# A hybrid encoder layer on one core: the high parts of the mixer's weights asked for one chunk further ahead, and another order inside the seven-product pairs

## The chip, the cores and the metric

One core of a Trainium2 chip. The metric is the device time of one execution in microseconds (us); lower is better. A difference under 0.3% is about what a measurement of this kernel can't tell from no change.

## The reference: what is computed

One encoder layer on 512 tokens of width 1024, all in float32:

```
h = rms_norm(x, g_mix);  z = h @ w_in            # split into latents, gates, values
a = mla(...)                                     # 4 heads of latent attention
r = hgrn2(...)                                   # 4 heads of a gated recurrence, both directions
x = x + concat(a, r) @ w_o
h = rms_norm(x, g_ffn)
x = x + (silu(h @ w_gate) * (h @ w_up)) @ w_down # inner width 2816 = 22 tiles of 128
x = x + sigmoid(rms_norm(x, g_ple) @ w_ple_gate) * (p @ w_ple_proj)
```

## The kernel before

Every float32 operand is kept as a high part (float32r) and a low part, the rest of it, and every product is three matmuls (`mm3`, L141 to L144): high by high, high by low, low by high. A weight therefore has to be loaded and split before TensorE can use it.

**Mixer.** The layer up to the residual of `w_o` runs as two streams of instructions that `merge` interleaves: a latency stream (attention, then the recurrence) and a dense stream (projections of 1024-column chunks of weights, the output projection, the embedding's projection). The dense stream takes its chunks from `wnext` (L602), which keeps `AHEAD` = 3 chunks prepared beyond the one in use. From the third chunk on a chunk is prepared without VectorE: GpSimd's queue (POOL) starts a DMA that casts the float32 weight into the high part `whi` (L155), ScalarE writes the negated high part into `wlo` (L156), and a second DMA of POOL's queue adds the float32 weight to it (L157). `whi` and `wlo` have `WB` = 4 buffers each, so a chunk's high part can be asked for when TensorE is done with the chunk four places before. Attention runs beside it; its softmax needs ScalarE (L557), and TensorE transposes the probabilities after it (L571). POOL also computes the small powers of every norm (L175).

**Feed-forward.** 22 pairs of a gate tile and an up tile. The first four are plain (`pair_plain`). After each of them `block_sums(c)` makes, from the normalised input, the sums that the other 18 pairs multiply by: in each half-width product the 1024 by 512 input is a 2 by 2 block matrix, and `pair_seven` gets the four blocks of its output from seven products instead of eight. A pair loads four raw blocks (A11 and A12 from `w_gate`, A21 and A22 from `w_up`, 256 KB each, L1102 on SyncE's queue, SP), forms four sums S1 to S4 of them on VectorE (`total`, L1112), splits all seven left operands (`operand`: high part on ScalarE L135, low part on VectorE L136) and runs seven products of twelve 128x256 matmuls (`product`), in the order A11, A12, S2, S1, S3, S4, A22. Between pairs run the down projections (`down`, tile `dn`).

**Buffers.** All 128x512 tiles of SBUF come from one list of numbered slots (`Slots`): `get` takes the slot that was put back longest ago, `put` appends. So the code alone fixes whose slot a tile inherits, and a load into it waits for that tile's last reader. There are `SLOTS` = 74, and 22 more (`SLOTS2`) once the mixer's weight buffers are closed.

**Order.** The order of the instructions of each engine is fixed at build time by the framework's scheduler, from its own times; each engine then runs in that order and stands wherever the next instruction is not ready.

Of the kernel before, what the change touches and what calls it, by code (L numbers as in the profile page):

```python
# [9 lines left out]
F32R = mybir.dt.float32r  # L10
I32 = mybir.dt.int32
AF = mybir.ActivationFunctionType
ALU = mybir.AluOpType
AX = mybir.AxisListType

P = 128
# [4 lines left out]
EPS = 1e-6  # L21
QK_SCALE = 192 ** -0.5
FPARTS = (4, 4, 4, 4, 3, 3)
SLOTS = 74
SLOTS2 = 22
DAHEAD = 2

# [1 line left out]
AHEAD = 3  # L29
WB = 4  # L30
# [4 lines left out]
LO_DVE = 2  # L35
# [76 lines left out]
def v3(t, a, b=None):  # L112

    return t.rearrange("p (a b) -> p a b", a=a)
# [3 lines left out]
def layer_kernel(ctx: ExitStack, tc: tile.TileContext, io, out):  # L118
    nc = tc.nc
    act, dve, pool, pe, sp = nc.scalar, nc.vector, nc.gpsimd, nc.tensor, nc.sync  # L120
# [6 lines left out]
    wpool = mixer.enter_context(tc.tile_pool(name="wpool", bufs=WB))  # L127
    A = Slots(spool, SLOTS, "u")
    B = Slots(ppool, 8, "b")


    def split(hi, lo, src, scale=None, eng=dve):

        if scale is None:
            act.activation(hi, src, AF.Copy)  # L135
            eng.tensor_tensor(lo, src, hi, ALU.subtract)  # L136
        else:
            act.activation(hi, src, AF.Copy, scale=scale)
            dve.scalar_tensor_tensor(lo, src, scale, hi, ALU.mult, ALU.subtract)

    def mm3(o, l, r, start, stop):  # L141
        pe.matmul(o, lhsT=l[0], rhs=r[0], start=start, stop=False)  # L142
        pe.matmul(o, lhsT=l[0], rhs=r[1], start=False, stop=False)  # L143
        pe.matmul(o, lhsT=l[1], rhs=r[0], start=False, stop=stop)  # L144

    nw = [0]

    def weights(src, cols, by_dma=False):


        nw[0] += 1
        hi = wpool.tile([P, 1024], F32R, tag="whi", name=f"whi{nw[0]}")
        lo = wpool.tile([P, 1024], F32R, tag="wlo", name=f"wlo{nw[0]}")
        if by_dma:
            pool.dma_start(hi[:, :cols], src)  # L155
            act.activation(lo[:, :cols], hi[:, :cols].bitcast(F32), AF.Copy, scale=-1.0)  # L156
            pool.dma_start(lo[:, :cols], src, accum_op=ALU.add)  # L157
        else:
            raw = wpool.tile([P, 1024], F32, tag="raw", bufs=RAWB, name=f"raw{nw[0]}")
            sp.dma_start(raw[:, :cols], src)  # L160
            split(hi[:, :cols], lo[:, :cols], raw[:, :cols])
        return hi, lo

    def cut(hl, a, b):
        return hl[0][:, a:b], hl[1][:, a:b]
# [123 lines left out]
    def load_k(k):  # L289

        if k:
            sp.dma_start(xT[k], io["xT"][k])
        raw = wpool.tile([P, 1024], F32, tag="raw", bufs=RAWB, name=f"rawl{k}")
        hi = wpool.tile([P, 1024], F32R, tag="whi", name=f"whil{k}")
        lo = wpool.tile([P, 1024], F32R, tag="wlo", name=f"wlol{k}")
        sp.dma_start(raw[:, :256], io["w_q"][:, k * 256 : k * 256 + 256])
        if k == 0:
            sp.dma_start(vec, io["vec"])
        if k == 1:
            sp.dma_start(pos, io["pos"])  # L300
            sp.dma_start(cst[:, C_FREQ:], io["cst"][:, C_FREQ:])
        sp.dma_start(raw[:, 256:576], io["w_kv"][:, k * 320 : k * 320 + 320])
        for c in (slice(0, 256), slice(256, 576)) if k == 0 else (slice(0, 576),):
            split(hi[:, c], lo[:, c], raw[:, c])
            if c.start == 0:
                split(hT[k][0], hT[k][1], xT[k], vec[:, V_MIX + k : V_MIX + k + 1])
        ws.append((hi, lo))
# [10 lines left out]
    for k in range(KT):  # L318
        load_k(k)
        query_k(k)  # L320
        if k == 1:
            rotary_tables()
        squares(sq, xT[k], k == 0)
        if k < KT - 2:
            key_k(k)
# [271 lines left out]

    wlist = deque()
    ahead = deque()
    nd = [0]  # L600

    def wnext():  # L602
        while wlist and len(ahead) < AHEAD:
            nd[0] += 1
            ahead.append(weights(*wlist.popleft(), by_dma=nd[0] > LO_DVE))
        return ahead.popleft()

    def w_in_tile(d):

        w = wnext()  # L610
        o = BD.get("wi")
        for k in range(KT):
            mm3(o, cut(w, k * P, k * P + P), hT[k], k == 0, k == KT - 1)
            if k % 2:
                yield 1.3
        z = A.get("z")
        dve.tensor_tensor(z, o, bc1, ALU.mult)
        BD.put(o)
        d.append(z)

    def w_in_tokens(evacuate):

        for half in range(2):
            ws = [wnext(), wnext()]
            for jp in range(2):
                o = [BD.get("wt0"), BD.get("wt1")]
                for c in range(2):
                    for k in range(4 * c, 4 * c + 4):
                        a = (k % 4) * 256
                        for i in range(2):  # L630
                            j = 2 * jp + i
                            mm3(o[i][:, :256], cut(hT[k], j * P, j * P + P), cut(ws[c], a, a + 256), k == 0, k == KT - 1)
                        if k % 2:
                            yield 1.3
                for i in range(2):
                    evacuate(2 * jp + i, slice(half * 256, half * 256 + 256), o[i][:, :256])
                BD.put(*o)
# [458 lines left out]
    def pair_seven(f):  # L1096


        r = {}
        for n, name, i in (("A11", "w_gate", 0), ("A21", "w_up", 0), ("A22", "w_up", 1), ("A12", "w_gate", 1)):  # L1100
            r[n] = A.get(n)
            sp.dma_start(r[n], io[name][f][:, i * 512 : i * 512 + 512])  # L1102

        def operand(n):
            hl = (A.get("whi", F32R), A.get("wlo", F32R))
            split(hl[0], hl[1], r[n])
            A.put(r[n])
            return hl

        def total(n, a, b, op):  # L1110
            r[n] = A.get(n)
            dve.tensor_tensor(r[n], r[a], r[b], op)  # L1112

        def product(o, hl, n):
            for c in range(4):
                mm3(o, cut(hl, c * P, c * P + P), blocks[n][c], c == 0, c == 3)
            A.put(*hl)

        total("S1", "A21", "A22", ALU.add)
        total("S2", "S1", "A11", ALU.subtract)  # L1120
        total("S3", "A11", "A21", ALU.subtract)
        A.put(r["A21"])
        total("S4", "A12", "S2", ALU.subtract)
        o12, o6, o75, o43 = (B.get(n) for n in ("p12", "p6", "p75", "p43"))
        L, R = slice(0, HB), slice(HB, S)
        product(o12[:, L], operand("A11"), "B11")
        product(o12[:, R], operand("A12"), "B21")
        product(o6[:, L], operand("S2"), "T2")
        product(o75[:, R], operand("S1"), "T1")
        product(o75[:, L], operand("S3"), "T3")  # L1130
        product(o43[:, R], operand("S4"), "B22")
        product(o43[:, L], operand("A22"), "T4")
        e, u, w = A.get("e"), A.get("u2"), A.get("u34")

        act.copy(u[:, R], o12[:, L])
        dve.tensor_tensor(u[:, L], o6[:, L], u[:, R], ALU.add)
        dve.tensor_tensor(e[:, L], o12[:, R], u[:, R], ALU.add)
        dve.tensor_tensor(v3(w, 2), v3(o75, 2), u[:, L].unsqueeze(1).broadcast_to([P, 2, HB]), ALU.add)
        dve.tensor_tensor(e[:, R], o75[:, R], w[:, L], ALU.add)
        dve.tensor_tensor(w, o43, w, ALU.add)  # L1140
        A.put(u)
        B.put(o12, o6, o75, o43)
        act.activation(e[:, L], e[:, L], AF.Silu)
        act.activation(w[:, R], w[:, R], AF.Silu)
        dve.tensor_tensor(e, e, w, ALU.mult)
        hl = (A.get("ah", F32R), A.get("al", F32R))
        split(hl[0], hl[1], e)
        A.put(e, w)
        return hl
# [40 lines left out]
    f = 0  # L1190
# [17 lines left out]
    for part, nf in enumerate(FPARTS):  # L1208
        acts[part] = []
        n = 0  # L1210
        for i in range(nf):
            acts[part].append(pair_seven(f) if part else pair_plain(f))
            f += 1
            if part == 0:
                block_sums(i)
                if i:
                    ask()
            else:
                while n < (i + 1) * KT // nf:
                    next_down()  # L1220
                    n += 1
        if part == 0:
            for hl in h2:
                A.put(*hl)
            A.put(bc2)
# [7 lines left out]
    for m in range(KT):  # L1233
        w = halves(io["w_pg"][m])

        n = 2 if m == KT - 1 else 1
# [90 lines left out]
```

## Time and profile before

| | us |
|---|---|
| median of 3 runs | 702.0 (700.14 to 702.2) |
| the profiled execution | 700.41 |
| its span, first to last instruction | 698.6 |
| TensorE busy in the span | 686.4 |
| VectorE / ScalarE / GpSimd busy | 509.5 / 383.2 / 111.1 |

The profiled execution is one more run of the same kernel, beside the three timed ones; 1.8 us of it lie outside the span. TensorE's granted clock is full in all of the 40 slices of the profile. Busy time of TensorE is modelled and includes overlap of matmuls, so what is read below are the places in which it stood idle and what ended the wait.

### The profile page before, as it was taken

Reading aid. Unit: us, or ns where it says so; the run is one execution under the profiler, and the core shown is the slowest. Engines: PE = TensorE matmul, PEld = TensorE weight load, DVE = VectorE, ACT = ScalarE, POOL = GpSimd, SP = SyncE. Lnnn points to the kernel's source line nnn. Section 1 sums busy time; section 2 is a strip of 40 time slices with the busy share of each in tenths; the row PEclk is TensorE's granted clock in tenths of the full one; section 3 lists DMA queues with packets and bytes.
Section 4 is the critical chain, followed back from the end, with each engine's and each line's share of the span. In section 5 each row is a group of like instructions: output and inputs, shape, how many; then the busy total and the mean of one; then the engine's idle time right before and its main releaser. Section 6 shows DMA issues by size and latency. Waiting matters only on the chain.

```text
span 698.6 us, 11350 instructions
## 1 busy us (share of the span) xinstructions
PE 686.4 (98%) x4170; PEld 604.2 (86%) x4170; DVE 509.5 (73%) x1031; ACT 383.2 (55%) x808; POOL 111.1 (16%) x144
## 2 busy tenths in 40 slices
PE   9999999899999999999989999999999999999997
PEld 8888887699878888878788999999999999998886
DVE  6944489797987943679987977877677578768663
ACT  7857795686645645535544554445544545546421
POOL 6233421101212222010111100001100110100000
PEclk9999999999999999999999999999999999999999
DMA  7575555543657657322456456345655664563111
GB/s 241 164 171 136 124 145 97 119 86 84 157 123 208 156 138 189 90 66 61 147 129 163 115 145 178 92 115 145 166 130 130 158 138 123 123 179 112 55 60 61
DMA packets 44264, 91.18 MB, mean 131 GB/s; under 512 B 5424, under 2 KB 11568, under 8 KB 44208
## 3 DMA queue, kind: packets, MB, share of 16 engines
q0 software_dynamic: 14976, 41.43, 28.8%
q1 hardware_dynamic: 29232, 49.02, 22.3%
q8 instruction: 33, 0.54, 0.3%
q14 instruction: 23, 0.19, 0.1%
HBM read 88.33 MB, written 2.10 MB: 129 GB/s over the span
## 4 chain that ended last, share of the span: by engine, by line
PE 86%; issue 8%; DMA 2%; ACT 2%; POOL 1%; DVE 1%; SPq 0%; POOLq 0%; ACTq 0%
PE p L144 8%; PE p L143 8%; PE p L142 8%; PE dn L143 5%; PE dn L144 5%; PE dn L142 5%; PE wi L143 4%; PE wi L142 4%; PE wi L144 4%; PE pg L144 2%; PE pg L142 2%; PE pg L143 2%; PE wo L142 2%; PE wo L144 2%; PE wo L143 2%
## 5 line engine op out<-in xcount | busy, mean ns | idle before, releaser
L142 PE MATMUL p<-bh,whi 128*128 128x256 f32 x432 | 122.3, 284 | 2.4 <-ACT whi L135 2.3
L143 PE MATMUL p<-bl,whi 128*128 128x256 f32 x432 | 121.8, 283 | 0.0
L144 PE MATMUL p<-bh,wlo 128*128 128x256 f32 x432 | 121.3, 283 | 0.0
L142 PEld LDWEIGHTS p<-bh,whi 128*128 128x128 f32 x432 | 82.7, 192 | 3.3 <-ACT whi L135 3.2
L143 PEld LDWEIGHTS p<-bl,whi 128*128 128x128 f32 x432 | 82.8, 192 | 0.1
L144 PEld LDWEIGHTS p<-bh,wlo 128*128 128x128 f32 x432 | 82.5, 192 | 0.1
L143 PE MATMUL dn<-al,whi 128*128 128x512 f32 x176 | 68.7, 390 | 0.0
L144 PE MATMUL dn<-ah,wlo 128*128 128x512 f32 x176 | 68.5, 389 | 0.0
L142 PE MATMUL dn<-ah,whi 128*128 128x512 f32 x176 | 67.7, 390 | 0.0
L1170 POOL DMA_DIRECT2D wlo<-in_w_d x32 | 27.4, 877 | 202.4 <-ACT wlo L1169 160.5
L1112 DVE TENSOR_TENSOR S<-A,A 128x512 f32<-128x512 f32 x36 | 24.4, 689 | 40.0 <-DMA A<-in_w_up 19.5
L135 ACT ACTIVATE whi<-A 128x512 fp32r<-128x512 f32 x54 | 33.6, 626 | 35.0 <-DMA A<-in_w_gate 22.8
L142 PE MATMUL wi<-hh,whi 128*128 128x512 f32 x128 | 51.2, 400 | 0.0
L144 PE MATMUL wi<-hh,wlo 128*128 128x512 f32 x128 | 50.9, 397 | 0.0
L143 PE MATMUL wi<-hl,whi 128*128 128x512 f32 x128 | 50.5, 394 | 0.0
L135 ACT ACTIVATE whi<-S 128x512 fp32r<-128x512 f32 x72 | 42.6, 623 | 10.3 <-DVE S L1112 9.0
L156 ACT ACTIVATE wlo<-whi 128x1024 fp32r<-128x1024 f32 x28 | 29.7, 1060 | 33.4 <-DMA whi<-in_w_hf 12.0
L136 DVE TENSOR_TENSOR wlo<-S,whi 128x512 fp32r<-128x512 f32 x72 | 46.3, 681 | 1.0 <-ACT whi L135 1.0
L135 ACT ACTIVATE whi<-raw 128x512 fp32r<-128x512 f32 (+2 forms) x42 | 25.5, 625 | 31.6 <-DMA raw<-in_w_up 9.7
L136 DVE TENSOR_TENSOR wlo<-A,whi 128x512 fp32r<-128x512 f32 x54 | 36.8, 682 | 3.1 <-ACT whi L135 3.1
L144 PEld LDWEIGHTS dn<-ah,wlo 128*128 128x128 f32 x176 | 33.1, 188 | 6.9
L142 PEld LDWEIGHTS dn<-ah,whi 128*128 128x128 f32 x176 | 33.0, 188 | 6.4
(342 smaller groups left out, 1840.6 us busy)
## 6 DMA issues: line engine op xcount, KB each, us to landing
A<-in_w_gate SPq DMA_DIRECT2D x36, 256.0 KB, 4.4
A<-in_w_up SPq DMA_DIRECT2D x36, 256.0 KB, 3.8
wlo<-in_w_d POOLq DMA_DIRECT2D x32, 256.0 KB, 5.3
whi<-in_w_hf POOLq DMA_DIRECT2D x14, 512.0 KB, 4.6
wlo<-in_w_hf POOLq DMA_DIRECT2D x14, 512.0 KB, 5.7
raw<-in_w_d SPq DMA_DIRECT2D x24, 256.0 KB, 2.8
x<-in_xT SPq DMA_DIRECT2D x16, 256.0 KB, 4.4
raw<-in_w_pg SPq DMA_DIRECT2D x16, 256.0 KB, 3.5
```

Of the source, the lines that this page charges most:

```text
L135: act.activation(hi, src, AF.Copy)
L136: eng.tensor_tensor(lo, src, hi, ALU.subtract)
L142: pe.matmul(o, lhsT=l[0], rhs=r[0], start=start, stop=False)
L143: pe.matmul(o, lhsT=l[0], rhs=r[1], start=False, stop=False)
L144: pe.matmul(o, lhsT=l[1], rhs=r[0], start=False, stop=stop)
L156: act.activation(lo[:, :cols], hi[:, :cols].bitcast(F32), AF.Copy, scale=-1.0)
L1112: dve.tensor_tensor(r[n], r[a], r[b], op)
L1170: pool.dma_start(lo[:, n], src, accum_op=ALU.add)
```

## The change

Two parts, and what they share.

1. In the mixer the high part of a chunk is started by a function of its own (`high`), and `wnext` starts it one chunk before the rest: of the chunks beyond the one in use three are complete or being completed, and a fourth has its casting DMA started. For this `whi` has one buffer more (`WB + 1` = 5; `wlo` keeps 4), in `load_k` as well, which shares the tag.
2. `pair_seven` loads its blocks in the order A11, A12, A22, A21 (before: A11, A21, A22, A12) and runs its products in the order A11, A12, A22, S1, S2, S3, S4. The sums are formed only after the products of raw blocks have been written down; A11 and A12 are put back after S3 and S4 instead of after their split.
3. The buffer of part 1 takes two slots: `SLOTS` = 72.

```diff
-SLOTS = 74
+SLOTS = 72
...
+    def high(src, cols):
         nw[0] += 1
-        hi = wpool.tile([P, 1024], F32R, tag="whi", name=f"whi{nw[0]}")
+        hi = wpool.tile([P, 1024], F32R, tag="whi", bufs=WB + 1, name=f"whi{nw[0]}")
+        pool.dma_start(hi[:, :cols], src)
+        return hi
+
+    def weights(src, cols, hi=None):
+        by_dma = hi is not None
+        if not by_dma:
+            nw[0] += 1
+            hi = wpool.tile([P, 1024], F32R, tag="whi", bufs=WB + 1, name=f"whi{nw[0]}")
         lo = wpool.tile([P, 1024], F32R, tag="wlo", name=f"wlo{nw[0]}")
         if by_dma:
-            pool.dma_start(hi[:, :cols], src)
             act.activation(lo[:, :cols], hi[:, :cols].bitcast(F32), AF.Copy, scale=-1.0)
             pool.dma_start(lo[:, :cols], src, accum_op=ALU.add)
...
     def wnext():
-        while wlist and len(ahead) < AHEAD:
+        while wlist and len(ahead) + len(highs) <= AHEAD:
+            c = wlist.popleft()
             nd[0] += 1
-            ahead.append(weights(*wlist.popleft(), by_dma=nd[0] > LO_DVE))
+            highs.append((*c, high(*c)) if nd[0] > LO_DVE else c)
+            if len(highs) > 1 or nd[0] <= LO_DVE:
+                ahead.append(weights(*highs.popleft()))
+        if len(ahead) < AHEAD and highs:
+            ahead.append(weights(*highs.popleft()))
         return ahead.popleft()
...
-        for n, name, i in (("A11", "w_gate", 0), ("A21", "w_up", 0), ("A22", "w_up", 1), ("A12", "w_gate", 1)):
+        for n, name, i in (("A11", "w_gate", 0), ("A12", "w_gate", 1), ("A22", "w_up", 1), ("A21", "w_up", 0)):
...
-        total("S1", "A21", "A22", ALU.add)
-        total("S2", "S1", "A11", ALU.subtract)
-        total("S3", "A11", "A21", ALU.subtract)
-        A.put(r["A21"])
-        total("S4", "A12", "S2", ALU.subtract)
...
-        product(o12[:, L], operand("A11"), "B11")
-        product(o12[:, R], operand("A12"), "B21")
+        product(o12[:, L], operand("A11", False), "B11")
+        product(o12[:, R], operand("A12", False), "B21")
+        total("S1", "A21", "A22", ALU.add)
+        product(o43[:, L], operand("A22"), "T4")
+        total("S2", "S1", "A11", ALU.subtract)
+        product(o75[:, R], operand("S1"), "T1")
+        total("S3", "A11", "A21", ALU.subtract)
+        A.put(r["A21"], r["A11"])
+        total("S4", "A12", "S2", ALU.subtract)
+        A.put(r["A12"])
         product(o6[:, L], operand("S2"), "T2")
-        product(o75[:, R], operand("S1"), "T1")
         product(o75[:, L], operand("S3"), "T3")
         product(o43[:, R], operand("S4"), "B22")
-        product(o43[:, L], operand("A22"), "T4")
```

## Rows read from the trace of the kernel before

**Rows 1.** Busy time of each engine over the span, from the page.

```profile
PE 686.4 (98%) x4170; PEld 604.2 (86%) x4170; DVE 509.5 (73%) x1031; ACT 383.2 (55%) x808; POOL 111.1 (16%) x144
```

**Rows 2.** Busy time by stretch: length, then each engine, clock, DMA share, GB/s.

```profile
120.00:130.00 10.00, 7.47 (x38) 4.93 (x36) 7.17 (x26) 4.27 (x12) 2.27 (x3) 1.00 0.46 107
...
320.00:330.00 10.00, 10.00 (x45) 8.27 (x45) 10.00 (x21) 4.06 (x9) 0.00 (x0) 1.00 0.20 28
...
340.00:360.00 20.00, 17.36 (x108) 14.72 (x109) 18.21 (x33) 11.24 (x21) 3.38 (x5) 1.00 0.60 159
360.00:640.00 280.00, 279.84 (x1909) 260.75 (x1908) 210.25 (x365) 139.60 (x271) 32.48 (x39) 1.00 0.55 138
640.00:699.00 59.00, 53.82 (x264) 45.45 (x262) 35.88 (x65) 19.44 (x33) 1.04 (x1) 0.99 0.19 67
```

**Rows 3.** Waits of TensorE over the span: us in total, times, longest.

```profile
PE pT L571 <- ACT p L557: 2.5, 2, 2.4
PE p L142 <- ACT whi L135: 2.3, 2, 1.2
```

**Rows 4.** Timeline from 119 to 130 us: start, duration, engine, instruction, idle before.

```profile
119.74 0.85 POOL L157 DMA_DIRECT2D wlo<-in_w_i  x1 [8.61 <-ACT wlo L156]
120.29 1.13 POOL L155 DMA_DIRECT2D whi<-in_w_i  x1
...
126.66 0.39 PE L142 MATMUL wi<-hh,whi 128*128 128x512 f32 x1
127.62 1.06 ACT L156 ACTIVATE wlo<-whi 128x1024 fp32r<-128x1024 f32 x1 [2.44 <-issue]
128.58 0.67 ACT L557 ACTIVATE p<-s,mx 128x512 f32<-128x512 f32 x1
...
129.40 0.55 PE L571 MATMUL pT<-cst,p 128*128 128x128 f32 x3 [2.35 <-ACT p L557]
```

**Rows 5.** DMA issues from 119 to 128 us: size, us from issue to landing.

```profile
wlo<-in_w_i POOLq DMA_DIRECT2D x1, 512.0 KB, 5.6
whi<-in_w_i POOLq DMA_DIRECT2D x1, 512.0 KB, 7.3
```

**Rows 6.** Waits of POOL's queue from 30 to 290 us.

```profile
POOL wlo L157 <- ACT wlo L156: 88.7, 22, 8.8
...
POOL whi L155 <- PE wt L144: 18.9, 3, 12.2
```

**Rows 7.** Timeline from 343 to 356 us, TensorE and ScalarE at the stalls.

```profile
343.79 0.39 PE L144 MATMUL p<-b11h,wlo 128*128 128x256 f32 x1 [0.26 <-DVE wlo L136]
...
350.04 0.39 PE L142 MATMUL p<-bh,whi 128*128 128x256 f32 x1 [1.11 <-ACT whi L135]
...
355.45 0.39 PE L142 MATMUL p<-bh,whi 128*128 128x256 f32 x1 [1.24 <-ACT whi L135]
...
349.36 0.63 ACT L135 ACTIVATE whi<-A 128x512 fp32r<-128x512 f32 x1 [0.98 <-DMA A<-in_w_gate]
...
354.77 0.63 ACT L135 ACTIVATE whi<-A 128x512 fp32r<-128x512 f32 x1 [3.22 <-DMA A<-in_w_gate]
```

**Rows 8.** Loads of raw blocks from 330 to 360 us: count, ns, first and last start; landing.

```profile
L1102 SPq DMA_DIRECT2D A<-in_w_gate x4: 328/328/394, 336.4 to 347.8; - x4
L1102 SPq DMA_DIRECT2D A<-in_w_up x4: 327/328/384, 341.0 to 347.3; - x4
...
DMA to landing us min/median/max: 2.6/3.9/7.0
```

**Rows 9.** Waits of SP's queue from 335 to 346 us.

```profile
SPq L1102 <- DVE bl L136: 6.9, 3, 4.2
...
SPq L1102 <- DVE b11l L136: 1.2, 1, 1.2
```

**Rows 10.** Timeline of VectorE from 343 to 346 us: the last low part of the block sums.

```profile
344.86 0.68 DVE L136 TENSOR_TENSOR bl<-t,bh 128x512 fp32r<-128x512 f32 x1
```

**Rows 11.** Busy time of the products' instructions (tile `p`) from 360 to 640 us.

```profile
360.00:640.00 280.00, 175.38 (x1435) 174.50 (x1433) 45.32 (x88) 6.08 (x17) 1.00 0.55 138
```

More of the change, by code (lines that the diff above doesn't have):

```diff
@@ L146, in layer_kernel @@
     nw = [0]
-    def weights(src, cols, by_dma=False):
+    def high(src, cols):
         nw[0] += 1
-        hi = wpool.tile([P, 1024], F32R, tag="whi", name=f"whi{nw[0]}")
+        hi = wpool.tile([P, 1024], F32R, tag="whi", bufs=WB + 1, name=f"whi{nw[0]}")
[6 more added lines that the diff above has]
+            hi = wpool.tile([P, 1024], F32R, tag="whi", bufs=WB + 1, name=f"whi{nw[0]}")
         lo = wpool.tile([P, 1024], F32R, tag="wlo", name=f"wlo{nw[0]}")
         if by_dma:
-            pool.dma_start(hi[:, :cols], src)
             act.activation(lo[:, :cols], hi[:, :cols].bitcast(F32), AF.Copy, scale=-1.0)
@@ L293, in load_k @@
         raw = wpool.tile([P, 1024], F32, tag="raw", bufs=RAWB, name=f"rawl{k}")
-        hi = wpool.tile([P, 1024], F32R, tag="whi", name=f"whil{k}")
+        hi = wpool.tile([P, 1024], F32R, tag="whi", bufs=WB + 1, name=f"whil{k}")
         lo = wpool.tile([P, 1024], F32R, tag="wlo", name=f"wlol{k}")
@@ L599, in layer_kernel @@
     ahead = deque()
+    highs = deque()
     nd = [0]
     def wnext():
-        while wlist and len(ahead) < AHEAD:
+        while wlist and len(ahead) + len(highs) <= AHEAD:
+            c = wlist.popleft()
             nd[0] += 1
-            ahead.append(weights(*wlist.popleft(), by_dma=nd[0] > LO_DVE))
+            highs.append((*c, high(*c)) if nd[0] > LO_DVE else c)
[3 more added lines that the diff above has]
+            ahead.append(weights(*highs.popleft()))
         return ahead.popleft()
@@ L1099, in pair_seven, with operand @@
         r = {}
-        for n, name, i in (("A11", "w_gate", 0), ("A21", "w_up", 0), ("A22", "w_up", 1), ("A12", "w_gate", 1)):
+        for n, name, i in (("A11", "w_gate", 0), ("A12", "w_gate", 1), ("A22", "w_up", 1), ("A21", "w_up", 0)):
             r[n] = A.get(n)
             sp.dma_start(r[n], io[name][f][:, i * 512 : i * 512 + 512])
-        def operand(n):
+        def operand(n, last=True):
             hl = (A.get("whi", F32R), A.get("wlo", F32R))
             split(hl[0], hl[1], r[n])
-            A.put(r[n])
+            if last:
+                A.put(r[n])
             return hl
```

## The prediction

> **What bounds the kernel now.** First the busy times: TensorE is busy for 686.4 of 698.6 us, VectorE for 509.5 [rows 1]. So the kernel is bound by TensorE, nothing in this change takes work from TensorE, and all that can be won is time in which TensorE stands: 12.2 us. Then the busy times by stretch, to see where that is. The last stretch lacks 5.2 us (0.4 of them lie beyond the span); they are the tail of the embedding's gate, which the change doesn't touch. Of the rest, 2.53 us are missing between 120 and 130 us and 2.64 between 340 and 360; in the 280 us after that, where nearly all seven-product pairs run, 0.16 are missing altogether [rows 2]. What is left, some 2.1 us, lies scattered before 120 us and between 130 and 340; I expect nothing of it. The waits of TensorE name the two holes: 2.4 us for ScalarE's softmax in the mixer, 2.3 us in two waits for a high part of a product's left operand [rows 3]. So the change has 5.2 us to win at most, plus what small stalls lie at their edges.
>
> **The hole in the mixer.** ScalarE works in order. At 127.62 it starts the negated copy into `wlo` (L156) after 2.44 us of idleness, and only behind it, at 128.58, the softmax for which TensorE has stood since 126.66 plus one matmul; TensorE goes on at 129.40 [rows 4]. The page puts no releaser to ScalarE's wait ("issue"). The DMA issues do: the high part asked for at 120.29 takes 7.3 us to land, thus until 127.59, 0.03 us before ScalarE moves [rows 4, 5]. It was asked for 0.55 us behind the accumulating DMA of the chunk before, another 512 KB in the same queue, and that one had held POOL for 8.61 us until ScalarE had written its `wlo` [rows 4]. So this is a chain of POOL, DMA and ScalarE and the softmax only stands in ScalarE's queue behind it.
>
> *Edit: high part one chunk earlier.* It adds no instruction and no byte: the same DMAs and copies, in another order in POOL's and ScalarE's queues. With five `whi` buffers chunk n+4 is asked for when chunk n-1 is done, where before it was chunk n+3; a chunk's DMA so gains the time of one chunk. A chunk of `w_in` is 24 matmuls of 512 columns, each 0.222 us where 45 of them fill 10 us [rows 2], thus 5.3 us at least, and more with attention between. The wait lasted 2.44 us, less than that. So the wait for the landing goes: **-2.5 us**. Bounds: -2.5, and 0, if ScalarE then waits in the same place for something else: the copy still needs the `wlo` buffer that chunk n-1 frees, and it can only go when TensorE is through with that. I take the whole gain: the high part's DMA at 120.29 goes without a wait of its own [rows 4], so the chunk whose buffers it takes was done with by then, seven us before ScalarE moved. What is late next: nothing in this stretch, whose other waits are tenths.
>
> The Trainium skill (DMA: Bandwidth & Descriptors, Anatomy of one DMA) fits the time of such a DMA by 2.0 us and one more per 436 KB, which for 512 KB is an estimate of 3.2 us. By it the high part would have landed at 123.5, before ScalarE stood, the wait would have another cause, and this term would be 0, the sum 2.5 us higher. The trace has 7.3 us for this one, so the measurement decides against it here.
>
> *POOL.* Its queue waits 88.7 us in 22 waits for ScalarE before accumulating DMAs, and 18.9 in three, 12.2 the longest, for TensorE to free a `whi` buffer [rows 6]. The high part moves one place forward in this queue, past the accumulating DMA of the chunk before it and past whatever powers of norms (L175) stand between. I cost that at 0, because the dense stream's prepared chunks feed TensorE meanwhile; without that cover it is the third rival below.
>
> **The hole at the first seven-product pairs.** At 343.79, 350.04 and 355.45 TensorE stands for 0.26, 1.11 and 1.24 us; before the last two ScalarE itself had idled 0.98 and 3.22 us for a load from `w_gate` [rows 7]. Which load? The code gives each tile its slot. The four blocks of the first such pair inherit the tiles of `block_sums(2)`: A11 its `xa`, A21 `xb`, A22 `t12`, A12 `t34`. SP waits there for VectorE's low parts of just these tiles, 4.2 us the longest [rows 9]. The last of those low parts ends at 344.86 + 0.68 = 345.54 [rows 10]; with the median landing of 3.9 us [rows 8] a load released by it lands at 349.4, and 349.36 is when ScalarE moves. So the first pair's A12 is what the stall of 1.11 us ends on. The second pair's blocks inherit slots of the normalised input, free when the last plain tile is done; its last load is issued at 347.8 and lands, after 7.0 us, at 354.8 [rows 8], which is when ScalarE moves for the last time [rows 7]: again A12, as it is the last in the old order.
>
> *Edit: the order of the loads.* The second pair's A12 becomes its second load. The last two go out at 347.3 and 347.8 [rows 8]. Issued no later than 347.3 and with two loads of 256 KB fewer in front of it, at the median landing of 3.9 us it is there at 351.2 instead of 354.8, before TensorE starts to stand (355.45 - 1.24 = 354.21). The 1.24 us go.
>
> *Edit: two slots fewer.* With these every `get` inherits what was put two puts later. For the first pair, counted out in the code in the new load order: A11 gets `t12`, A12 gets `t34` as before, A22 and A21 get the raw buffers of the fourth plain pair's gate tile, free long before. So A12 is no earlier than before (345.54 plus the landing), and A11, which was asked for at 336.4, is asked for at about 341.0, when the slot that A22 had is free [rows 8, 9].
>
> *Edit: the order of the products.* What TensorE can do until A12 lands: A22 and A21 now come early, and the products of A22 and S1 need no A12. A product is 12 matmuls of 175.38/1435 = 0.122 us, 1.47 us [rows 11]. Either fills the 1.11 us, if the scheduler puts it there. Against it, the product of A11 is no longer at hand before about 345 (341.0 + 3.9), where it had been filler. I take half of the 1.11 and half of the 0.26. **-1.24 - 0.55 - 0.13 = -1.9 us**. Bounds: -2.6, if all go, and +1.5, if the first A11 product leaves a hole of its length.
>
> *The sums on VectorE, the splits:* same count and size; only their order changes. In the later pairs TensorE has no hole (0.16 us in 280 [rows 2]), so the new order there is worth 0: what hides it is the lead of the loads. Of the 33 slots or so that a pair and its down tiles turn over, by the code, two fewer take a sixteenth of that lead; were the cover gone, the price would be a stall like those of [rows 7] in each of 17 pairs.
>
> *Slots in the mixer.* Counted through the code, at the tightest place (gates and attention, just behind the hole at 120 us) 5 slots are free, now 3. A `get` there waits for a reader two puts later. No row prices it; the nearest are SP's waits on slots, 6.9 us in three [rows 9], and they didn't reach TensorE whole. I take **+0.4 us**, bounds 0 and 2.3 (one such wait, whole).
>
> **Sum.** -2.5 - 1.9 + 0.4 = -4.0 us, on the profiled execution's 700.41: 696.4. That execution is 1.6 us under the median of the three timed ones, whose lowest is 700.14 and highest 702.2; the four together have their middle at 701.2. So I add 0.8: **697.2 us** as the median to be measured.
>
> **Rivals.**
> *Only one of the holes closes.* For it: the slot of the first A12 is as late as before, and ScalarE's in-order wait may just change its reason. Then -2.5 + 0.4 or -1.9 + 0.4 on 701.2: 699.1 to 699.7.
> *The change does nothing to either.* The mixer's wait is not for the landing but for the `wlo` buffer, and the first pairs are set by VectorE, which is busy for 18.21 of the 20 us from 340 to 360 [rows 2]. Time: 700.4 to 702. The first half of this is what the Trainium skill's fit (DMA: Bandwidth & Descriptors, Anatomy of one DMA) would bring.
> *Slower: POOL's queue stands on the fifth buffer.* A high part asked for earlier sits at the head of POOL's in-order queue until TensorE frees a buffer; the accumulating DMA of the chunk that is needed next and the attention's powers wait behind it. The longest such wait today is 12.2 us [rows 6]. It decides once it outlasts the work that TensorE has at hand: with no more than one tile left (the 5.3 us from above), 12.2 - 5.3 = 6.9 us of standing, and with the gain of the pairs 701.2 - 1.9 + 0.4 + 6.9 = 706.6. Against it: the old order had the same wait on a buffer, and three prepared chunks ahead of it.
>
> **How the numbers follow.** Both holes close, wholly or mostly: 0.47, with 694.5 to 698.5 as its own range (5.2 us and a us of small change off the low runs, 2.7 off 701.2). One closes: 0.25. Neither: 0.17. Slower by POOL or by a new hole that the scheduler's other order leaves: 0.11. Faster by over 0.3% means under 699.9: all of the first, nearly all of the second: 0.69. Slower means over 704.1: 0.10. Same: 0.21. The range runs from 693.5, both holes and the small ones at their edges gone, to 702.5, where nothing came of it.
>
> **What would show it.** In the profile after: no wait of TensorE for the softmax near 125 us, and ScalarE's copies L156 starting without a wait for `whi`; TensorE's missing time from 340 to 360 at 0.7 us instead of 2.6; still next to none after 360. The prediction is wrong if TensorE's new waits, wherever they are, sum to as much as the two holes, or if ScalarE stands at L156 for TensorE.

## The result, and the profile after

| | before | after |
|---|---|---|
| median, us | 701.71 (700.14 to 702.2, 4 runs) | 693.32 (692.36 to 693.84, 4 runs) |
| the profiled execution, its span | 700.41, 698.6 | 692.36, 690.6 |
| TensorE busy, matmuls | 686.4, 4170 | 682.4, 4170 |

The ratio is 0.9865, with an interval of 0.9831 to 0.9898: 8.4 us faster, about twice the forecast and just under its range. The busy times from the page of the changed kernel answer to [rows 1]:

```profile
PE 682.4 (99%) x4170; PEld 604.9 (88%) x4170; DVE 509.6 (74%) x1031; ACT 388.1 (56%) x808; POOL 109.6 (16%) x144
```

The span is 8.0 us shorter, and TensorE's idle time only 4.0 (12.2 to 8.2). The other 4.0 were counted as work: the same 4170 matmuls now take 682.4 us of modelled busy time instead of 686.4. The stretches, in the columns of [rows 2]:

```profile
120.00:130.00 10.00, 10.00 (x52) 8.25 (x51) 8.85 (x34) 6.13 (x14) 1.41 (x2) 1.00 0.58 126
...
340.00:360.00 20.00, 20.00 (x150) 19.17 (x149) 18.73 (x33) 12.79 (x23) 3.26 (x5) 1.00 0.66 185
360.00:640.00 280.00, 280.00 (x1886) 260.03 (x1886) 210.63 (x366) 145.85 (x276) 32.77 (x39) 1.00 0.54 138
```

Both holes of [rows 2] are closed: nothing is missing from 120 to 130 us nor from 340 to 360. TensorE's waits, as in [rows 3], without one of 1.0 at the very start:

```profile
PE ff L142 <- ACT whi L135: 1.2, 1, 1.2
...
PE wo L142 <- ACT ppo L967: 0.8, 1, 0.8
```

Where the time came from is seen best in two milestones, the last start of the output projection's matmuls (`wo`, the mixer's end) and of the products' (`p`), in the rows of these tiles; the columns are count, ns of one (least, median, most), first and last start. Before:

```profile
L144 PE MATMUL wo<-rTh,wlo x32: 389/389/478, 273.4 to 295.0; 128*128 128x512 f32 x32
L144 PE MATMUL p<-bh,wlo x432: 274/283/283, 352.9 to 625.8; 128*128 128x256 f32 x144
```

After:

```profile
L144 PE MATMUL wo<-rTh,wlo x32: 387/389/482, 266.6 to 291.0; 128*128 128x512 f32 x32
L144 PE MATMUL p<-bh,wlo x432: 277/283/283, 343.4 to 617.8; 128*128 128x256 f32 x144
```

The mixer ends 4.0 us earlier, and the stretch from there to the last product is 326.8 us long instead of 330.8, another 4.0. What follows is the same. Below, the first milestone is "the mixer's end" and the second distance "the products' stretch". "Lost" is the time from the start of each matmul to the next one's beyond its usual distance (0.227 us for 512 columns, 0.120 for 256, and so on), summed with the shorter distances counted against it, in the mixer from 32 us on; each is from one profiled execution. Lost in the mixer: 7.0 us before, 2.8 after.

What ScalarE's negated copies waited for in the mixer (25 to 292 us): idle time before line 156 of the kernel before, us and times, and who waited for the copies:

```profile
  DMA whi<-in_w_hf: 12.0, 7
  DMA whi<-in_w_oa: 7.8, 3
  DMA whi<-in_w_pp: 3.8, 1
  DMA whi<-in_w_or: 3.7, 3
  PE pk L814: 2.8, 1
  issue: 2.4, 1
  DMA whi<-in_w_i: 0.4, 1
...
  POOL wlo L157: 88.7, 22
```

The same copies after, now line 164:

```profile
  PE wi L144: 5.7, 5
  PE wt L143: 4.0, 3
  PE wo L144: 2.9, 2
  DMA whi<-in_w_hf: 1.7, 1
...
  POOL wlo L165: 30.7, 24
```

The wait behind the hole at 126 us is the row "issue", 2.4. Beside it ScalarE stood 15 more times for a high part, 27.7 us by the five rows that name a DMA, and 1.7 now. POOL's wait for ScalarE fell with them, 88.7 to 30.7 us. In exchange POOL stands for a free `whi` buffer much longer than in [rows 6]; its queue after, from 30 to 290 us:

```profile
POOL whi L152 <- PE wi L144: 58.8, 13, 9.2
POOL whi L152 <- PE wt L144: 35.3, 4, 20.3
```

That is the mechanism of the third rival, with a longest wait of 20.3 us, and it costs TensorE nothing that is seen: in its list of waits none is for a chunk.

### The profile page after: what moved, and what is told of

Its sections match the earlier page's. It is cut to its first block, busy times and chain, and to the rows that moved or that the text cites. A ratio compares the mean times of both kernels' runs of the same rounds, so it can differ in the third digit from the quotient of the medians.

```text
span 690.6 us, 11392 instructions
## 1 busy us (share of the span) xinstructions
PE 682.4 (99%) x4170; PEld 604.9 (88%) x4170; DVE 509.6 (74%) x1031; ACT 388.1 (56%) x808; POOL 109.6 (16%) x144
## 4 chain that ended last, share of the span: by engine, by line
PE 94%; DVE 4%; DMA 1%; issue 0%; ACT 0%; SPq 0%; ACTq 0%
PE p L144 9%; PE p L143 9%; PE p L142 9%; PE dn L143 6%; PE dn L144 6%; PE dn L142 6%; PE wi L142 4%; PE wi L143 4%; PE wi L144 4%; PE pg L142 2%; PE pg L144 2%; PE pg L143 2%; PE wo L144 2%; PE wo L142 2%; PE wo L143 2%; PE po L852 1%
## 5 line engine op out<-in xcount | busy, mean ns | idle before, releaser
L135 ACT ACTIVATE whi<-S 128x512 fp32r<-128x512 f32 x72 | 44.8, 630 | 43.3 <-DVE S L1128 40.7
L136 DVE TENSOR_TENSOR wlo<-S,whi 128x512 fp32r<-128x512 f32 x72 | 48.3, 683 | 0.5 <-ACT whi L135 0.3
L136 DVE TENSOR_TENSOR wlo<-raw,whi 128x512 fp32r<-128x512 f32 (+2 forms) x42 | 28.3, 687 | 14.3 <-ACT whi L135 14.0
L143 PEld LDWEIGHTS dn<-al,whi 128*128 128x128 f32 x176 | 33.1, 188 | 6.2
```

## The experiments

**One part at a time.** The first edit takes the old `pair_seven` and keeps the rest of the change; the second only the new `pair_seven`; the third only two slots fewer; the fourth the third with the new `pair_seven`.

```diff
# mixer_only: the changed kernel with the old pair_seven
# pairs_only: the kernel before with the new pair_seven
# slots_only, pairs_72: the kernel before, pairs_only, with
-SLOTS = 74
+SLOTS = 72
```

> Part 1 and the two slots fewer, with the old order inside the pairs. In the profile after, the mixer's last output-projection matmul starts 4.0 us earlier (291.0 against 295.0 us), and the rest up to the last product is another 4.0 us shorter. Theory (each part closes its own hole, the parts add up): the first 4.0 us come, 697.7 us, the holes at the first seven-product pairs stay. Rival (what pays is another order of the scheduler, which any edit draws anew): the mixer's gain is not 4.0 but anything, and the pairs, untouched, change by us as well. Rival (only the wait of 2.5 us goes): 699.2 us.

> Part 2 alone, with 74 slots and the old mixer. Theory (the parts add up): the mixer ends where it did, at 295 us, the pairs win 4.0 us, 697.7 us. Rival (two slots fewer are what moved the loads of the first pairs, since A22 and A21 then inherit tiles that are free long before): the holes at 350 and 355 us stay in part and the gain is 1 to 2 us, 700 us. Rival (scheduler's order): anything.

> The kernel before with 72 slots in place of 74, nothing else. Theory (parts add up, slots cost little): 701.7 to 702.5 us. Rival (the slots moved the loads at the first pairs): a gain of 1 to 3 us between 340 and 360 us, 699 to 700.5 us. Rival (scheduler's order): anything within 5 us, with the mixer's end moved as well.

> Part 2 and the two slots fewer, with the old mixer. Theory (parts add up): 697.7 us, as with 74 slots. Rival (slots moved the loads): better than with 74 slots by 1 to 3 us, and together with the part of the mixer alone it gives the whole 8.4. Rival (scheduler's order): differs from the run with 74 slots by us in places that neither edit touches.

| | median, us | ratio to before, interval | mixer's end | products' stretch |
|---|---|---|---|---|
| before | 701.70 | | 295.0 | 330.8 |
| mixer_only | 693.41 | 0.9885 [0.9864, 0.9907] | 291.0 | 327.4 |
| pairs_only | 698.56 | 0.9957 [0.9941, 0.9973] | 294.7 | 328.1 |
| slots_only | 704.29 | 1.0029 [1.0009, 1.0049] | 293.9 | 334.1 |
| pairs_72 | 700.94 | 0.9986 [0.9969, 1.0004] | 295.9 | 329.7 |

Each ratio here and below is to the kernel before as timed beside the run, with medians from 701.46 to 702.95.

Part 1 alone, with its two slots fewer, gives the whole gain, in the products' stretch too, which its code doesn't touch. Part 2 alone gives 3.1 us, and on top of part 1 nothing (693.41 to 693.32). The parts don't add up. Two slots fewer cost 2.6 us by themselves (2.0 by the ratio).

The hole before the softmax closes without the fifth buffer as well: TensorE's lists of waits in slots_only and pairs_72 have none for the softmax, though ScalarE's copies still stand 23.6 us there for high parts. So that this one hole is gone doesn't show what the buffer does; ScalarE's waits and the times of the next kernels do.

**Is it the earlier call or the fifth buffer?** Two kernels ask one chunk further ahead only for some chunks, and one has the fifth buffer and the 72 slots with the code of `wnext` as before.

```diff
# early_but_wor: a chunk further ahead only up to chunk 26; early_wor: only from 27 on (old pair_seven)
-        while wlist and len(ahead) + len(highs) <= AHEAD:
+        while wlist and len(ahead) + len(highs) < AHEAD + (nd[0] + 1 <= 26):
...
# buffer_only: the kernel before with (and the same in load_k)
-        hi = wpool.tile([P, 1024], F32R, tag="whi", name=f"whi{nw[0]}")
+        hi = wpool.tile([P, 1024], F32R, tag="whi", bufs=WB + 1, name=f"whi{nw[0]}")
...
-SLOTS = 74
+SLOTS = 72
```

> Part 1 (693.4 us by itself) with the early ask taken back for the last four chunks of the mixer, the lower half of the output projection, and kept for the 24 before; the scheduler writes almost the same order otherwise. Theory (the early ask works all along the mixer by freeing ScalarE of waits for a casting DMA, and the feed-forward's gain of 4 us comes from the last four chunks being ready sooner, so that the residual and the norm's squares are done before the mixer's last matmul): the mixer's gain stays but for about 1 us, the squares end 8 us later against the end of the output projection, the holes at the first seven-product pairs return, 696 to 698 us. Rival (the feed-forward's gain is only the scheduler's order there, which this edit leaves): 693.4 to 694 us.

> The opposite: five buffers, but the high part is asked for early only for the last four chunks. Theory: the mixer keeps its waits of ScalarE for casting DMAs (some 20 us in all) and ends no earlier than before, but the squares are done early and the feed-forward is as fast as with the whole part 1, 697 to 698 us. Rival (order): anything between 693 and 704.

> The fifth buffer for the high part and 72 slots, but nothing asked for earlier: what the buffer alone gives. Theory (the early ask is what pays): ScalarE's waits for casting DMAs stay at 20 to 30 us, 701 to 704 us, as with 72 slots alone (704.3). Rival (a fifth buffer lets the DMA go earlier by itself, when TensorE's release was what it waited for): ScalarE's waits fall and the time is under 698 us.

Measured: 693.51 (ratio 0.9864 [0.984, 0.9888]), 693.11 (0.9859 [0.9835, 0.9883]) and 693.74 (0.987 [0.9847, 0.9893]). All three are as fast as the whole change. In buffer_only, whose source calls as late as before, ScalarE's copies wait as in the changed kernel (line 156, from 25 to 292 us):

```profile
  PE wi L144: 5.1, 4
  DMA whi<-in_w_hf: 4.9, 1
  PE wt L143: 4.0, 3
  PE wo L144: 2.9, 2
```

In the traces POOL's queue holds the same instructions in the same order up to 285 us in the changed kernel, mixer_only and these three: with five buffers the scheduler placed the DMAs alike, wherever the source asks for them. So the place in the source did not matter here; the buffer did. The two kernels that ask early for some chunks only are thus no test of which chunks matter.

**Other slot counts.** Every tile inherits the slot put back longest ago, so one slot more or less changes every tile's predecessor and the order that the scheduler finds. mixer_73 is mixer_only, after_73 and after_71 the whole change, slots_73 the kernel before, and pairs_71 pairs_only, each with the count in its name.

```diff
-SLOTS = 72
+SLOTS = 73
```

> Part 1 alone with 73 slots instead of 72: an edit that moves every buffer's heir by one and draws the scheduler's order anew, with the same early ask. Theory (the gain is the early ask's): 692.5 to 695 us. Rival (the scheduler's order is what pays, and this one was a lucky draw): 696 us or more.

> The whole change with 73 slots instead of 72. Part 1 alone took 693.4 us with 72 slots and 700.7 with 73, where its mixer was as fast and the first seven-product pairs lost the time: a hole of 5 us at 348 us, in which ScalarE stands for the down projection's casting DMA ahead of the split that TensorE needs. Theory (the new order of the pairs is an insurance: the products of raw blocks give TensorE work where the order of the day leaves a hole): 696 to 698 us. Rival (the pairs' order does nothing by itself, what counts is the order that the scheduler draws): about 700.7, or anything else.

> The whole change with 71 slots: another draw of the scheduler's order with both parts in it. Theory (the fifth buffer's 4 us in the mixer come with any order, and the feed-forward's share is drawn): the mixer ends at 291 to 292 us, TensorE's missing time in it about 3 us; the whole lies between 693 and 698 us. Rival (the mixer's gain too was drawn): the mixer's missing time is 5 us or more.

> The kernel before with 73 slots instead of 74 and nothing else: the matched partner, with four buffers for the high parts, of mixer_73 (five buffers, 73 slots, 700.74). Theory A, the fifth buffer takes about 4 us out of the mixer at any slot count: the last matmul of wo ends near 295 us against 291.5 in mixer_73, ScalarE still waits some 25 to 30 us for high parts in the mixer, and the time is 704 to 706. Rival, the good order at 72 slots was luck and the buffer is worth nothing by itself: 699 to 702, the last matmul of wo near 292.

> The new pairs with four buffers and 71 slots: the matched partner of after_71 (five buffers, 71 slots, 705.67, whose mixer ended at 297.6 us). Theory A, the fifth buffer takes about 4 us out of the mixer at any slot count: the mixer ends near 301 us here and the time is 708 to 711. Rival, at 71 slots what limits the mixer is the slots and no longer the landing of high parts: the mixer ends within 1 us of 297.6 and the time is 704 to 707.

| `whi` buffers, slots, pairs | median, us | ratio to before, interval | mixer's end (lost) | products' stretch |
|---|---|---|---|---|
| mixer_73: 5, 73, old | 700.74 | 0.9969 [0.9954, 0.9985] | 291.5 (3.3) | 336.0 |
| slots_73: 4, 73, old | 708.53 | 1.0082 [1.0056, 1.0108] | 300.4 (13.0) | 333.4 |
| after_73: 5, 73, new | 696.98 | 0.9929 [0.9905, 0.9953] | 290.7 (2.4) | 329.7 |
| after_71: 5, 71, new | 705.67 | 1.0057 [1.0037, 1.0077] | 297.6 (8.8) | 335.6 |
| pairs_71: 4, 71, new | 702.54 | 1.0005 [0.9981, 1.0029] | 297.9 (9.4) | 330.0 |

With 72 and 73 slots the fifth buffer is worth 7.6 to 10.9 us between kernels that differ in part 1 only (704.29 to 693.41, 708.53 to 700.74, 700.94 to 693.32; 7.9 to 10.1 by the ratios), and by itself as much (buffer_only against slots_only: 704.29 to 693.74). slots_73 is slower than theory and rival had it. The buffer fits beside 73 slots too, so it was not what took the second slot. The mixer ends at 290.7 to 291.5 us in the profiles of the tables that have it, 293.1 in buffer_only's. With 71 slots theory A fell: the mixer's end stays (297.9, 297.6) and the time rises by 3.1 us. The whole change is slower there than the kernel before (705.67 against 701.46). So the 8.4 us of the change are in part the luck of 72 slots. Yet the waits for high parts are nearly gone with 71 too. pairs_71, before line 156:

```profile
  DMA whi<-in_w_hf: 14.9, 8
  DMA whi<-in_w_oa: 7.0, 2
  DMA whi<-in_w_i: 6.8, 2
...
```

after_71, before line 164, and then two of TensorE's waits, both in the mixer:

```profile
  PE wo L144: 5.1, 3
  DMA whi<-in_w_hf: 3.0, 1
```

```profile
PE pq L142 <- ACT kt L464: 1.8, 1, 1.8
PE pT L579 <- ACT p L565: 1.3, 1, 1.3
```

ScalarE's wait for the landings falls (28.7 us by the three rows, and 3.0), but TensorE stands in the mixer for ScalarE's other work: for `kt`, a wait that pairs_71 doesn't have, and for the softmax as in pairs_71 (1.4 there). Its longest waits in after_71 are behind the mixer, 3.2 us for the norm's squares and 2.4 for a split, against 1.4 and 2.1 in pairs_71. Over all profiles with 71 to 74 slots, ScalarE's copies stand 23.6 to 40.2 us for high parts with four buffers, by the rows that name a DMA, and 1.7 to 6.9 with five. So the buffer takes most of that wait away at each count; whether TensorE gains by it depends on the order that is drawn.

**The hole at the first pairs.** mixer_73 loses in the products' stretch what the mixer won. Its timeline (start, duration, engine, instruction, idle before it):

```profile
352.05 0.63 ACT L1176 ACTIVATE wlo<-whi 128x512 fp32r<-128x512 f32 x1 [4.50 <-DMA whi<-in_w_d]
352.58 0.61 ACT L135 ACTIVATE whi<-A 128x512 fp32r<-128x512 f32 x1
...
353.25 0.58 PE L142 MATMUL p<-b11h,whi 128*128 128x256 f32 x1 [5.02 <-ACT whi L135]
```

and of POOL's queue just ahead of it:

```profile
343.90 0.86 POOL L1177 DMA_DIRECT2D wlo<-in_w_d  x1 [4.51 <-ACT wlo L1176]
344.45 0.88 POOL L1175 DMA_DIRECT2D whi<-in_w_d  x1
```

The chain of [rows 4] at another place: an accumulating DMA that had waited for ScalarE, the casting DMA right behind it, which takes 7.6 us until 352.05, ScalarE in order behind its landing, and behind ScalarE's copy the split that TensorE needs. Three edits of mixer_73 tested this against a rival, VectorE's backlog there.

```diff
# dahead3_73: the down projection's weights are asked for one step further ahead
-DAHEAD = 2
+DAHEAD = 3
# relief_sq_73: the adds of the norm's squares before the feed-forward go from VectorE to GpSimd
...
-            squares(sqacc, xT[m], m == 0)
+            squares(sqacc, xT[m], m == 0, pool if g == V_FFN else dve)
# nocast_73, and nocast_after on the changed kernel: part 0 of w_down loaded raw by SyncE, split as other parts are
-        if part == 0:
+        if part < 0:
```

> Part 1 with 73 slots (700.7 us) and the down projection's weights asked for three tiles ahead instead of two, DAHEAD = 3. Theory (the hole of 5 us at its first pairs is the mixer's case over again: ScalarE in order behind a casting DMA that lands late): ScalarE's wait for the down projection's high part falls from 4.5 us to under 1, and the time to 694 to 697 us. Rival (the hole is VectorE's backlog of block sums): the hole stays, 700 us or more.

> Part 1 with 73 slots (700.7 us) and the seven additions of the feed-forward norm's squares moved from VectorE to GpSimd; hardly anything else in the order changes. Theory (VectorE's backlog at the start of the feed-forward is what delays the block sums and opens the holes): the last low part of the block sums ends 4 us earlier after the mixer's last matmul, and the time falls by 3 to 5 us. Rival (the hole is ScalarE behind the casting DMA): the hole at 348 us stays and the time is 699.5 to 701.

> mixer_73 with the first part's down-projection weights loaded raw by SyncE and split as in the later parts, instead of by a casting DMA for which ScalarE stands in order. Theory: the 5.2 us hole of mixer_73 at 348 us ends on ScalarE's wait for that casting DMA (4.5 us), so it goes, with the lower clock behind it: 695 to 697. Rival: VectorE's backlog at the first pairs sets that place and the splits of the raw tiles add to it: 699 to 703, the hole still there with another name.

> The changed kernel with the same edit (first part's down-projection weights raw, by SyncE). The changed kernel has no hole at that place, so by both theories there is little to win: 692.5 to 694.5. If the order drawn for the scheduler changes for the worse, as it did with one slot more, it is 696 to 701.

Measured: dahead3_73 701.55 (1.0001 [0.9982, 1.002]), relief_sq_73 702.22 (1.0 [0.9981, 1.0018]), nocast_73 700.23 (0.9971 [0.995, 0.9992]), nocast_after 695.37 (0.9903 [0.9878, 0.9927]). In the first two the hole stays, 4.3 and 4.4 us from start to start beyond the usual (5.2 in mixer_73), and ScalarE still stands for the casting DMA, up to 4.4 and 5.5 us. dahead3_73 came out as the rival had it, but that DMA went out only 2 us earlier (342.36), so the edit hardly did what it was for. relief_sq_73 didn't relieve VectorE as meant: the last low part of its block sums starts 51.5 us after the mixer's end, against 49.8, so it tells little of the rival, which stays open. Without the casting DMA the hole is gone: the products wait 0.3 us there. But plain pairs now stand, in nocast_73's waits from 300 to 370 us:

```profile
PE ff L142 <- ACT whi L135: 2.0, 1, 2.0
PE ss L192 <- DVE sq L218: 1.4, 1, 1.4
...
PE p L144 <- DVE wlo L136: 0.3, 1, 0.3
```

Its profiled execution is 4.5 us shorter than mixer_73's (697.64, 702.12), but it is the fastest of its runs, and the median is only 0.5 lower. The timeline and this run speak for the casting DMA as the hole's cause, but the edit redraws the order as well, so it isn't isolated; closing the hole won almost nothing in the median. The time of its twelve runs goes with their mean granted clock: 0.999 in the profiled one, 0.992 in the slowest (703.95 us). What TensorE did before the clock fell in the runs without a profile stays open. nocast_after is 2 us slower than the changed kernel: no version here is clearly better than that one.

**Which half of the pairs' edit?** Loads in the new order and products in the old, and the reverse, with 74 slots and four buffers.

```diff
# pairs_loads
-        for n, name, i in (("A11", "w_gate", 0), ("A21", "w_up", 0), ("A22", "w_up", 1), ("A12", "w_gate", 1)):
+        for n, name, i in (("A11", "w_gate", 0), ("A12", "w_gate", 1), ("A22", "w_up", 1), ("A21", "w_up", 0)):
# pairs_prods: the new products and sums, the old line of loads
```

> The kernel before with only the new order of the four loads of a seven-product pair (A11, A12, A22, A21); products, slots and buffers as before. pairs_only (loads and products) measured 698.56 against 701.7. Theory as in the prediction, that the late landing of A12 makes the holes at the first pairs: the second pair's hole of 1.24 us goes, the first pair's of 1.11 us stays or shrinks: 699.5 to 700.8. Rival, the order of the products does it: 701.2 to 702.2, the holes at 350 and 355 us as before.

> The kernel before with only the new order of the products of a seven-product pair; loads (A12 last), slots and buffers as before. Theory that the loads' order matters: A12 lands as late as before and is needed second instead of fifth, so the holes stay or grow: 701 to 703. Rival, that the products' order gives the gain, because work is at hand that needs only what has landed: 698.5 to 700.

Measured: pairs_loads 701.25 (0.9987 [0.9966, 1.0008]), pairs_prods 700.55 (0.9981 [0.9954, 1.0009]); neither can be told from before by its time. The traces differ. pairs_loads still stands at the first pairs, as its timeline shows:

```profile
350.46 0.39 PE L142 MATMUL p<-bh,whi 128*128 128x256 f32 x1 [0.84 <-ACT whi L135]
352.12 0.38 PE L144 MATMUL p<-bh,wlo 128*128 128x256 f32 x1 [0.59 <-DVE wlo L136]
354.44 0.58 PE L142 MATMUL p<-bh,whi 128*128 128x256 f32 x1 [0.66 <-ACT whi L135]
```

In pairs_prods one wait is left between 338 and 357 us, where the kernel before has 2.6 in all and pairs_loads 2.4:

```profile
346.66 0.39 PE L142 MATMUL p<-bh,whi 128*128 128x256 f32 x1 [1.02 <-ACT whi L135]
```

The products' stretch is 332.6 us with the new loads alone and 328.4 with the new products alone (330.8 before, 328.1 with both). But the 332.6 hold a fall of TensorE's granted clock behind these stands, which the profile of the kernel before doesn't have (the columns of [rows 2]):

```profile
353.20:360.00 6.80, 6.14 (x27) 5.63 (x26) 6.43 (x12) 4.20 (x9) 0.00 (x0) 0.50 0.21 55
```

So go by the waits: in these profiles the order of the products closes most of them, that of the loads hardly any. That pairs_prods gains little in all is put down in its profile to the mixer, which ends at 297.2 us, 2.2 later than before, with code that the edit didn't touch. The hole before the softmax is there as before, 2.4 us, but behind it the clock fell, which it didn't before. The kernel before, then pairs_prods:

```profile
129.50:133.00 3.50, 3.50 (x19) 2.79 (x20) 3.11 (x7) 2.21 (x5) 0.88 (x2) 1.00 0.75 125
129.50:133.00 3.50, 3.50 (x11) 2.66 (x11) 2.39 (x5) 1.28 (x3) 0.55 (x1) 0.51 0.92 149
```

11 matmuls run there instead of 19. The rest of the 2.2 us is in part a wait of 1.1 for `pp`.

## Why the prediction was wrong, step by step

**The cap.** "So the change has 5.2 us to win at most" is the first step that failed. It took modelled busy time for work. The same 4170 matmuls then took 4.0 us less of it: TensorE's late starts were in part covered by the modelled ends of the matmuls before them. Counted from start to start, 14.9 us were lost before and 6.9 are after. The Trainium skill (Perfetto Trace Analysis, Identifying the Most-Contended Engine) warns that the busy share of matmuls is a poor measure of how near a kernel is to its limit, because they are pipelined, and names the share of the weight loads, beside the FLOPs, as a better one. The trace agrees: the loads kept their 604.2 us (604.9 after), so their share rose from 86 to 88%, while the matmuls' busy time fell by 4.0.

**The hole in the mixer, -2.5: the mechanism right for ScalarE's wait, the size too small.** The wait for the landing goes, as predicted, and TensorE no longer stands for the softmax; the mixer's end moves by 4.0 us. The fifth buffer does it, and not the earlier call that the change was named for; and slots_only closes the softmax hole with four buffers, so its going is no proof of the step. Between kernels with 72 slots the mixer ends 2.9 us earlier with the buffer (slots_only 293.9, mixer_only 291.0). Of the 4.2 us less that are lost, the hole and two short stalls just ahead of it are 3.0; a new wait for `ppo` takes some 1.3 back; the rest, 2.4, are distances of under 0.12 us each, which I couldn't put down to single causes. The step summed one wait that TensorE saw, and not ScalarE's others. Of the signs named for this hole, no wait of TensorE for the softmax held, and the copies' waits for `whi` are down to one, of 1.7 us; the copies do wait for TensorE, 12.6 us by the rows above, which the text named as a sign of being wrong, but it costs TensorE nothing that is seen.

The Trainium skill (DMA: Bandwidth & Descriptors, Anatomy of one DMA) gave an estimate of 3.2 us for such a landing, and the rival built on it would have left the hole as it was. The high parts land in 3.5 to 8.1 us, median 4.8, in the mixer of the kernel before and in 3.5 to 7.0, median 4.0, in the changed kernel's: all later than the estimate, so the measurement decided rightly against that rival.

**The pairs, -1.9: the wrong cause credited.** The products' stretch did shorten by 4.0 us, but 3.4 of them come with mixer_only (330.8 to 327.4). There the holes don't arise, with the old pairs: the reading is that the scheduler draws another order, but what in it closes them isn't isolated. That the stretch of the changed kernel came out shorter, as forecast, is luck as far as the edit of the pairs goes. The edit itself is worth 3.1 us with 74 slots and four buffers, 3.4 with 72 and four, 3.8 with 73 and five (2.8 by the ratios), and 0.1 where it was used: it mends holes that an order leaves, if it leaves any. Within the edit, I gave 1.24 us to the loads' order and about 0.7 to the products'; the waits in the traces of the halves say the reverse (2.4 and 1.0 us left of 2.6), the times can't tell.

**The slots, +0.4 with an upper bound of 2.3: mis-sized.** Alone two slots fewer cost 2.6 us (interval of the ratio 1.0009 to 1.0049), one slot fewer 5.6 (708.53 against 702.95). I priced a wait on a slot; what changes is the whole order, and with 72 slots it happens to lack the hole before the softmax and to have others. The largest single wait in slots_73 is TensorE's 5.8 us at 361 us for a split, with ScalarE idle for 5.4 before it for a casting DMA of `w_down`. With five buffers and 72 slots nothing of this is seen.

**The rivals.** None came true. POOL does stand on the fifth buffer, up to 20.3 us, but TensorE shows no wait for a chunk, so nothing says that its condition (no more than one tile at hand) came about. What no part of the forecast had was that an edit in the mixer shortens the feed-forward by as much as the mixer.

## What to carry to other kernels

An engine that works in order and must wait for a DMA holds up everything queued behind it, so sum all its waits for that DMA and not the one that the bound engine shows; one more buffer took most of them away here, and the earlier call in the source was not needed. Don't cap a gain by modelled busy time: count distances from start to start. Where a scheduler and a ring of slots fix the order, a change of one buffer or slot moved this kernel by 2 to 12 us in places that the edit doesn't name, so time neighbouring counts before an edit gets the credit.

## What the runs showed that I had not expected

**The clock after a stand.** After some stands of TensorE its granted clock was lower: behind 2.8 us in slots_only (0.48 of them busy) it was 0.96 for 1.8 us and then 0.52 for 3.4. In slots_73 it fell during the stand and stayed low behind it, by stretch (the columns of [rows 2]):

```profile
348.00:354.80 6.80, 6.80 (x44) 6.18 (x43) 6.30 (x11) 3.59 (x6) 1.43 (x2) 1.00 0.70 178
354.80:361.00 6.20, 0.35 (x4) 0.15 (x2) 2.65 (x5) 1.24 (x3) 0.32 (x1) 0.69 0.53 144
361.00:364.00 3.00, 3.00 (x13) 3.00 (x14) 3.00 (x6) 2.85 (x7) 0.54 (x1) 0.51 0.53 80
```

A clock of 0.51 is the 1.2 GHz level. TensorE's timeline there has matmuls of 256 columns 0.21 us apart, where before the stand they are 0.12:

```profile
354.60 0.28 PE L143 MATMUL p<-bl,whi 128*128 128x256 f32 x1
354.72 0.28 PE L142 MATMUL p<-bh,whi 128*128 128x256 f32 x1
...
361.35 0.41 PE L143 MATMUL p<-b11l,whi 128*128 128x256 f32 x1
361.56 0.41 PE L144 MATMUL p<-bh,wlo 128*128 128x256 f32 x1
```

13 matmuls at 0.09 us more each are 1.2 us on top of the 5.8 of the wait. From 364 us on the clock is 1.00 again. The hole at 126 us shows no such fall in the profile of the kernel before [rows 2], and does in that of pairs_prods above: a hole can cost more than its length, and not each time.

**The spread.** The kernels at 693 us repeat within 2 us (the changed kernel 692.36 to 693.84, mixer_only 693.02 to 694.65). Most kernels with holes at the first pairs spread over more (mixer_73 699.29 to 703.01, the kernel before 698.66 to 706.14 beside slots_73). slots_73 itself, with the longest hole, does not (707.04 to 708.98). The spread goes with the granted clock. Of the 125 runs of the kernel before that were timed beside the experiments, the 16 with a mean clock of 1.000 have a median of 700.74 us, the 13 with 0.994 or less one of 703.76; in nocast_73 the four fastest runs (697.64 to 699.45) have 0.997 to 1.000, the four slowest (700.87 to 703.95) 0.992 to 0.996. The kernels at 693 us, with hardly a hole, have 0.998 to 1.000 in all their runs. So a hole seems to cost a second time through the clock, in some executions and not in others. In the runs without a profile that isn't shown; there only the two numbers go together.
